# Rows of four transposes merged in pairs in a two-layer hybrid encoder kernel

## Chip, cores and metric

The kernel runs on one core of a Trainium2 chip. The metric is the device time of one execution in microseconds (us). Before the change the median of three runs is 1239.62 us (1239.03 to 1239.73).

## What is computed

Two layers of a macaron encoder on 256 tokens of width 1024, all in float32. Cut to what matters here:

```
for l in range(2):
    x = x + 0.5 * swiglu(rms_norm(x, g1), w1, w3, w2)
    h = rms_norm(x, gm);  z = h @ w_in
    y_na, y_gla, y_mla = three token mixers on slices of z
    mixed = sum_i sigmoid(gate_i) * (y_i @ w_br_i)
    x = x + mixed @ w_out
    x = x + 0.5 * swiglu(rms_norm(x, g2), w1, w3, w2)
```

Every product needs its left side with the contracted dimension on the partitions, so activations that were computed with tokens on the partitions are transposed in 128x128 blocks: x before each norm's product, the compressed inputs and the queries and keys inside the mixers, and `mixed` before `w_out`.

## The kernel before

**Split operands.** A float32 value is kept as a pair: a high part rounded to fp32r (made on ScalarE, ACT) and a low part, the rest (made on VectorE, DVE). A product is three passes of TensorE (PE): high x high, high x low, low x high. Weights arrive by DMA in units of 128x2048 and are split in halves of 128x1024: `emit_hi` (L143, ACT) and `emit_lo` (L149, DVE). The activations' pairs lie in `xT` (token block t, high or low, eight 128-wide blocks k).

**Tokens** come in two blocks, t = 0 and 1; a row of x is handled in halves of 512 columns, h = 0 and 1.

**Order.** No scheduler moves anything: every engine runs its instructions in the order in which the Python code emits them. `tick()` is called after each block of matmuls (most often 12 of 512 columns). It calls `fill()`, which emits pending weight splits, and then advances each live task (a Python generator) by one step; `spawn(gen, wait)` sets after how many ticks the task's first step comes, `yield n` sets the next. `finish(task)` emits what is left of it at once. With `tick(True)` the tasks come ahead of `fill()`. So a row of transposes that a task emits falls between two blocks of matmuls on PE, and its evictions fall behind the weight splits that ACT and DVE were given before.

**Transposes.** A row of four 128x128 transposes fills one PSUM bank (`tr_t`, tag `ta`, four banks shared with other uses). The rows that the change touches:

- `norm_task` (L257 to L277): one task for each half row of x. Four transposes (L264), four scaled copies into the high part (L267, ACT), four subtractions for the low part (L271, DVE), the sum of squares (L274). It stands at the end of each feed-forward block's last product (`wide_out`, x is updated at L554) and of the mixer's last product (x updated at L1229). Five norms run this way.
- `c_task` (L607 to L620): the transposes of the compressed inputs, one row for j = 0, one for j = 1, with a yield between them (L616).
- `na_tr` (L705 to L717): neighbourhood queries and keys, two rows each (L699).
- `mix_task` (L1206 to L1214): in `branch`, the third branch's product of block (h, t) is multiplied by its gate and added to `mixed` (L1200 and L1202, both on DVE for this branch); `mix_task` then transposes the block (L1211) and splits it into `xT` by `split_bank`: L247 on ACT, then L248 on DVE. The product with `w_out` (`wide_out`, `wide_burst`) follows at once. Its first 12 matmuls read block t = 0 of half h = 0: four with the high part, then two with the low part, and so on.

All products go through one helper, `mm` (L370), so the trace shows them under that line.

Of the kernel before, what the change touches and what calls it, by code (L numbers as in the profile page):

```python
# [6 lines left out]
F32 = mybir.dt.float32  # L7
# [3 lines left out]
AF = mybir.ActivationFunctionType  # L11
ALU = mybir.AluOpType
# [34 lines left out]
def body(tc, T):  # L47
# [3 lines left out]
    with ctx:  # L51
# [7 lines left out]
        PE, ACT, DVE, POOL = nc.tensor, nc.scalar, nc.vector, nc.gpsimd  # L59

        def s2(shape=(128, 512), dt=F32):
            return sp.tile(list(shape), dt, name="s2", tag="s2", bufs=S2_BUFS)

        def small(n, dt=F32, tag="sm", bufs=24):
            return sm.tile([128, n], dt, name=tag, tag=tag, bufs=bufs)

        def bank(tag, bufs):
            return pp.tile([128, 512], F32, name=tag, tag=tag, bufs=bufs)

        acc_t = lambda: bank("acc", 4)  # L70
        tr_t = lambda: bank("ta", 4)
# [90 lines left out]
        def unit():  # L162
            i = st["next"]
            st["next"] += 1
            split_to(2 * i + 3)
            return hls[i]
# [19 lines left out]
        def tick(fill_last=False):  # L186
            if not fill_last:
                fill()
            for tk in list(tasks):
                if tk.done:  # L190
                    continue
                tk.wait -= 1
                if tk.wait <= 0:
                    step(tk)
            if fill_last:
                fill()

        def spawn(gen, wait=1):
            tk = Task(gen, wait)
            tasks.append(tk)  # L200
            return tk

        def finish(tk):
            while not tk.done:
                step(tk)
# [7 lines left out]
        x = cst.tile([128, 2, D], F32, name="x")  # L213
        idt = cst.tile([128, 128], F32, name="idt")
        xT = cst.tile([128, 2, 2, 8, 128], F32R, name="xT")
# [27 lines left out]
        def junk(n):  # L243
            return sp.tile([128, 512], BF, name="junk", tag="junk", bufs=1)[:, :n]

        def split_bank(ps, hi, lo, n=512):
            ACT.activation(out=hi, in_=ps, func=AF.Copy)  # L247
            DVE.tensor_tensor(out=lo, in0=ps, in1=hi.bitcast(F32), op=ALU.subtract)  # L248
# [3 lines left out]
        rs_sq, rs_b, ss_x = {}, {}, {}  # L252

        def xdst(t, h):
            return [xT[:, t, w, 4 * h:4 * h + 4, :].rearrange("p k n -> p (k n)") for w in range(2)]

        def norm_task(t, h, G):  # L257
            sl = slice(h * 512, h * 512 + 512)
            if h == 0:
                ss_x[t] = small(2)  # L260
            yield 1
            ps = tr_t()
            for k in range(4):
                PE.transpose(ps[:, k * 128:(k + 1) * 128], x[:, t, h * 512 + k * 128:h * 512 + k * 128 + 128], idt)  # L264
            for k in range(4):
                kk = 4 * h + k
                ACT.activation(out=xT[:, t, 0, kk, :], in_=ps[:, k * 128:(k + 1) * 128], func=AF.Copy,  # L267
                               scale=G[:, kk:kk + 1])
            for k in range(4):
                kk = 4 * h + k  # L270
                DVE.scalar_tensor_tensor(out=xT[:, t, 1, kk, :], in0=ps[:, k * 128:(k + 1) * 128],  # L271
                                         scalar=G[:, kk:kk + 1], in1=xT[:, t, 0, kk, :].bitcast(F32),
                                         op0=ALU.mult, op1=ALU.subtract)
            ACT.activation(out=junk(512), in_=x[:, t, sl], func=AF.Square, accum_out=ss_x[t][:, h:h + 1])  # L274
            if h == 1:
                rs_tk[t] = spawn(rs_task(t))

        rs_tk = {}

        def rs_task(t):  # L280
            ss = ss_x[t]
            DVE.tensor_tensor(out=ss[:, 0:1], in0=ss[:, 0:1], in1=ss[:, 1:2], op=ALU.add)
            r = rs_x[t] = small(1)
            DVE.tensor_scalar(ss[:, 1:2], ss[:, 0:1], 1.0 / D, EPS, op0=ALU.mult, op1=ALU.add)  # L284
            POOL.tensor_tensor(out=r, in0=ss[:, 1:2], in1=mhalf[:, 0:1], op=ALU.pow)  # L285
            yield 1
            for count in (64, 256):
                q = rs_sq[t, count] = small(1)
                DVE.tensor_scalar(q, r, r, 1.0 / count, op0=ALU.mult, op1=ALU.mult)
# [274 lines left out]
        def mixer(l, norms, after, prefetch):  # L564
# [5 lines left out]
                                     op0=ALU.mult, op1=ALU.mult)  # L570
# [37 lines left out]
            def c_task(deps):  # L608
                for d in deps:
                    finish(d)  # L610
                yield 1
                for j in range(2):
                    ps = tr_t().rearrange("p (k t n) -> p k t n", k=2, t=2)
                    for t in range(2):
                        for k in range(2):
                            PE.transpose(ps[:, k, t, :], cn[t][:, j * 256 + k * 128:j * 256 + k * 128 + 128], idt)  # L616
                    hi, lo = s2(dt=F32R), s2(dt=F32R)
                    split_bank(ps.rearrange("p k t n -> p (k t n)"), hi, lo)
                    cT[j] = (hi, lo)
                    yield 1  # L620

            def ev_r(t, acc):
                r = rl[t] = small(160, tag="rl", bufs=2)
# [70 lines left out]
            def four(src, base):  # L694
                ps = tr_t().rearrange("p (k t n) -> p k t n", k=2, t=2)
                for t in range(2):
                    for k in range(2):
                        a = base + k * 128
                        PE.transpose(ps[:, k, t, :], src[t][:, a:a + 128], idt)  # L699
                return ps.rearrange("p k t n -> p k (t n)")  # L700
# [4 lines left out]
            def na_tr(nm, deps):  # L705
                for d in deps:
                    finish(d)
                yield 1
                for j in range(2):
                    ps = four([nqk[nm, 0], nqk[nm, 1]], j * 256)  # L710
                    o = naT[nm, j] = s2((128, 2, 256))
                    if nm == "q":
                        ACT.activation(out=o.rearrange("p k (c r) -> p k r c", r=4),
                                       in_=ps.rearrange("p k (r c) -> p k r c", r=4), func=AF.Copy, scale=gqk_na)
                    else:
                        DVE.tensor_copy(o, ps)
                    yield 1  # L717

            def na_chain(deps):
                for d in deps:  # L720
# [461 lines left out]
            mixed, mt = {}, {}  # L1182

            def branch(i, key):
                lh = lambda hl, k, t: yT[key, k // 2][hl][:, (k % 2) * 256 + t * 128:(k % 2) * 256 + t * 128 + 128]
                for h in range(2):
                    hl = unit()
                    for t in range(2):
                        acc = acc_t()
                        burst(acc, lh, hl, range(4), t, 512, True, True)  # L1190
                        if i < 2:
                            g = gates[:, t, i * 1024 + h * 512:i * 1024 + h * 512 + 512]
                        else:
                            g = late.pop((h, t))
                        if i == 0:
                            m = mixed[h, t] = s2()
                            DVE.tensor_tensor(out=m, in0=acc, in1=g, op=ALU.mult)
                        else:
                            m = mixed[h, t]
                            DVE.tensor_tensor(out=g, in0=acc, in1=g, op=ALU.mult)  # L1200
                            e = DVE if i == 2 else POOL
                            e.tensor_tensor(out=m, in0=m, in1=g, op=ALU.add)  # L1202
                        if i == 2:
                            mt[h, t] = spawn(mix_task(h, t), 3)
                        tick()

            def mix_task(h, t):
                m = mixed.pop((h, t))
                ps = tr_t()
                for k in range(4):  # L1210
                    PE.transpose(ps[:, k * 128:k * 128 + 128], m[:, k * 128:k * 128 + 128], idt)  # L1211
                split_bank(ps, *xdst(t, h))
                return
                yield  # L1214

# [18 lines left out]
        def spawner(ap, into, params_of=None):  # L1234
            G = []

            def f(t, h):
                into[t, h] = spawn(norm_task(t, h, G[0]), 1)

            def prefetch():  # L1240
                G.append(load_gain(ap))
                if params_of is not None:
                    load_params(params_of)
            return f, prefetch
# [3 lines left out]
        for l in range(DEPTH):  # L1248
            W = T["layers"][l]
            nm, n2 = {}, {}  # L1250
# [132 lines left out]
```

## Time and profile before

| | |
|---|---|
| median of three runs | 1239.62 us |
| profiled execution, its own time | 1239.52 us |
| its span in the trace | 1237.7 us |
| PE busy | 1233.5 us (100%) |
| DVE busy | 892.4 us (72%) |
| ACT busy | 710.9 us (57%) |
| POOL busy | 217.6 us (18%) |

A time of a run holds some 2 us around the span. The ends of matmuls are modelled, so a PE that shows 100% busy may still wait: a wait shows as a longer distance between starts, and on the row of the weight loads (PEld).

### The profile page before, as it was taken

The page shows a single profiled execution, that of the slowest core. Times are in us where ns is not written, and L with a number is a line of the kernel's source. Part 1 is how long each engine was busy: PE and PEld are TensorE (multiplying, and loading weights), DVE is VectorE, ACT ScalarE, POOL GpSimd, SP SyncE. Part 2 cuts the span into 40 slices and gives each one's busy share as a digit, 9 for nine tenths or more (in the row PEclk, how much of TensorE's full clock was granted, in tenths as well). Part 3 has the DMA queues.
Part 4 walks back from the last instruction along what each step waited for, and adds up shares of the span by engine and source line. Part 5 has one row for each costly group of instructions (what it writes and reads, how often), then busy time and mean ns, then how long its engine had stood idle before and what let it go on. Part 6 is the DMA issues. An engine that isn't in the chain of part 4 may idle for free.

```text
span 1237.7 us, 18188 instructions
## 1 busy us (share of the span) xinstructions
PE 1233.5 (100%) x7048; PEld 1061.4 (86%) x7048; DVE 892.4 (72%) x1399; ACT 710.9 (57%) x1317; POOL 217.6 (18%) x165
## 2 busy tenths in 40 slices
PE   9999999999999999999999999999999999999999
PEld 8888888889988888888888888888899888888887
DVE  6888837689667778886478886476896677788862
ACT  7665536567755465655356565356686654656541
POOL 0222102132112012220012220021322030122200
PEclk9999999999999999999999999999999999999999
DMA  8655744662554455557355556346525445555560
GB/s 332 211 202 177 252 150 162 224 195 93 187 190 146 173 200 178 201 177 249 119 204 207 191 195 247 108 172 238 176 99 201 171 142 190 188 195 189 186 238 34
DMA packets 37910, 228.58 MB, mean 185 GB/s; under 512 B 5760, under 2 KB 7040, under 8 KB 13376
## 3 DMA queue, kind: packets, MB, share of 16 engines
q1 hardware_dynamic: 37680, 227.42, 52.0%
q8 instruction: 55, 0.90, 0.3%
q14 instruction: 31, 0.25, 0.1%
q10 hardware_dynamic: 144, 0.00, 0.0%
HBM read 224.26 MB, written 1.05 MB: 182 GB/s over the span
## 4 chain that ended last, share of the span: by engine, by line
PE 100%; DVE 0%; issue 0%
PE acc L370 81%; PE ta L370 16%; PE ta L699 1%; PE ta L264 1%; PE ta L308 0%; PE ta L1211 0%; PE ta L684 0%; PE ta L737 0%; PE ta L616 0%; PE ta L1026 0%; PE ta L299 0%; PE ta L477 0%; PE ta L956 0%; DVE x L554 0%; DVE junk L305 0%
## 5 line engine op out<-in xcount | busy, mean ns | idle before, releaser
L149 DVE TENSOR_TENSOR hl<-raw,hl 128x1024 fp32r<-128x1024 f32 (+1 forms) x418 | 561.2, 1383 | 83.6 <-ACT hl L143 73.2
L143 ACT ACTIVATE hl<-raw 128x1024 fp32r<-128x1024 f32 (+1 forms) x418 | 412.8, 1040 | 103.4 <-PE ta L370 81.3
L370 PE MATMUL acc<-xT,hl 128*128 128x256 f32 (+1 forms) x2720 | 464.7, 332 | 0.0
L370 PEld LDWEIGHTS acc<-xT,hl 128*128 128x128 f32 x2720 | 407.6, 188 | 54.7
L370 PE MATMUL acc<-hl,xT 128*128 128x512 f32 (+1 forms) x1584 | 362.1, 384 | 0.0
L370 PEld LDWEIGHTS acc<-hl,xT 128*128 128x128 f32 x1584 | 291.9, 188 | 47.7 <-issue 1.7
L370 PE MATMUL acc<-hl,s 128*128 128x512 f32 x816 | 193.6, 390 | 0.0
L370 PEld LDWEIGHTS acc<-hl,s 128*128 128x128 f32 x816 | 152.5, 188 | 31.7 <-issue 0.3
L491 POOL TENSOR_TENSOR s<-s,rsb 128x512 f32<-128x512 f32 x79 | 109.5, 1387 | 352.4 <-DVE s L490 352.4
L370 PE MATMUL ta<-hl,s 128*128 128x512 f32 (+2 forms) x648 | 148.3, 378 | 0.0
L370 PEld LDWEIGHTS ta<-hl,s 128*128 128x128 f32 x648 | 117.6, 188 | 21.7
L500 ACT ACTIVATE s<-s 128x256 fp32r<-128x256 f32 x82 | 34.0, 417 | 168.2 <-DVE s L498 168.2
L490 DVE TENSOR_TENSOR s<-acc,s 128x256 f32<-128x256 f32 x158 | 59.7, 420 | 58.4 <-ACT s L489 58.4
L577 POOL TENSOR_TENSOR sm<-sm,mhalf 128x4 f32<-128x4 f32 (+2 forms) x24 | 36.7, 1531 | 192.0 <-DVE sm L581 192.0
L285 POOL TENSOR_TENSOR sm<-sm,mhalf 128x1 f32<-128x1 f32 x12 | 14.1, 1176 | 294.3 <-DVE sm L284 294.3
L489 ACT ACTIVATE s<-acc 128x256 f32<-128x256 f32 x158 | 50.6, 372 | 0.0
L248 DVE TENSOR_TENSOR s<-ta,s 128x512 fp32r<-128x512 f32 (+1 forms) x46 | 26.6, 604 | 30.0 <-ACT s L247 29.9
L267 ACT ACTIVATE xT<-ta,gain 128x128 fp32r<-128x128 f32 x80 | 22.8, 368 | 36.3 <-PE ta L264 36.3
L247 ACT ACTIVATE s<-ta 128x512 fp32r<-128x512 f32 (+1 forms) x46 | 22.9, 532 | 31.4 <-PE ta L699 16.9
L496 ACT ACTIVATE s<-s 128x256 f32<-128x256 f32 x82 | 34.2, 419 | 11.3 <-POOL s L491 0.3
L370 PE MATMUL ta<-s,s 64*64 64x128 f32 (+4 forms) x720 | 35.8, 260 | 0.0
L370 PEld LDWEIGHTS ta<-s,s 64*64 64x64 f32 (+3 forms) x720 | 30.4, 145 | 5.9 <-issue 4.2
(164 smaller groups left out, 676.6 us busy)
## 6 DMA issues: line engine op xcount, KB each, us to landing
raw<-in_l_f_w SPq DMA_DIRECT2D x123, 1024.0 KB, 4.8
raw<-in_l_in_g SPq DMA_DIRECT2D x16, 816.0 KB, 4.4
raw<-in_l_in_late SPq DMA_DIRECT2D x8, 1024.0 KB, 4.8
raw<-in_l_out SPq DMA_DIRECT2D x8, 1024.0 KB, 4.7
raw<-in_l_f_up SPq DMA_DIRECT2D x6, 1024.0 KB, 4.8
raw<-in_l_in_m SPq DMA_DIRECT2D x4, 1024.0 KB, 4.8
raw<-in_l_in_gr SPq DMA_DIRECT2D x4, 1024.0 KB, 4.8
raw<-in_l_in_r SPq DMA_DIRECT2D x4, 1024.0 KB, 4.8
```

The source lines that it names most:

```text
L143: ACT.activation(out=hls[j][:, 0, sl], in_=raws[j][:, sl], func=AF.Copy)
L149: DVE.tensor_tensor(out=hl[:, 1, sl], in0=r[:, sl], in1=hl[:, 0, sl].bitcast(F32), op=ALU.subtract)
L247: ACT.activation(out=hi, in_=ps, func=AF.Copy)
L248: DVE.tensor_tensor(out=lo, in0=ps, in1=hi.bitcast(F32), op=ALU.subtract)
L267: ACT.activation(out=xT[:, t, 0, kk, :], in_=ps[:, k * 128:(k + 1) * 128], func=AF.Copy, scale=G[:, kk:kk + 1])
L370: PE.matmul(out=out, lhsT=lhsT, rhs=rhs, start=start, stop=stop, skip_group_check=True)
L489: ACT.activation(out=g[:, j, :], in_=a[j][:, 256:], func=AF.Copy)
L490: DVE.tensor_tensor(out=g[:, j, :], in0=a[j][:, :256], in1=g[:, j, :], op=ALU.add)
L491: POOL.tensor_tensor(out=g, in0=g, in1=rb[:, None, :].to_broadcast([128, 2, 256]), op=ALU.mult)
L496: ACT.activation(out=g[:, 0, :], in_=g[:, 0, :], func=AF.Silu)
L500: ACT.activation(out=o[:, 0, :], in_=g[:, 0, :], func=AF.Copy)
L577: POOL.tensor_tensor(out=r[:, :n], in0=ss[:, :n], in1=mhalf[:, :n], op=ALU.pow)
```

## The change

Eighteen pairs of rows become rows of eight. In `norm_task` one task does both halves of a token block: eight transposes, then the evictions of both banks, then both sums of squares (five norms, two token blocks: ten pairs). In `c_task` the yield between the two rows goes (one pair a layer), in `na_tr` that of the queries (one pair a layer). In `mix_task` one task does both token blocks of a half h; it is spawned when t = 1 is done (two pairs a layer). No instruction is added or removed; the order on the engines changes.

```diff
-        def norm_task(t, h, G):
+        def norm_task(t, G):
...
-            ps = tr_t()
-            for k in range(4):
-                PE.transpose(ps[:, k * 128:(k + 1) * 128], x[:, t, h * 512 + k * 128:h * 512 + k * 128 + 128], idt)
...
+            pss = [tr_t() for _ in range(2)]
+            for h in range(2):
+                for k in range(4):
+                    PE.transpose(pss[h][:, k * 128:(k + 1) * 128],
+                                 x[:, t, h * 512 + k * 128:h * 512 + k * 128 + 128], idt)
+            for h, ps in enumerate(pss):
...
@@ c_task
                     cT[j] = (hi, lo)
-                    yield 1
+                yield 1
@@ na_tr
-                    yield 1
+                    if nm == "k" or j:
+                        yield 1
@@ branch
-                        if i == 2:
-                            mt[h, t] = spawn(mix_task(h, t), 3)
+                        if i == 2 and t:
+                            mt[h, 0] = mt[h, 1] = spawn(mix_task(h), 3)
@@ mix_task
-            def mix_task(h, t):
-                m = mixed.pop((h, t))
-                ps = tr_t()
-                for k in range(4):
-                    PE.transpose(ps[:, k * 128:k * 128 + 128], m[:, k * 128:k * 128 + 128], idt)
-                split_bank(ps, *xdst(t, h))
+            def mix_task(h):
+                pss = [tr_t() for _ in range(2)]
+                for t in range(2):
+                    m = mixed.pop((h, t))
+                    for k in range(4):
+                        PE.transpose(pss[t][:, k * 128:k * 128 + 128], m[:, k * 128:k * 128 + 128], idt)
+                for t in range(2):
+                    split_bank(pss[t], *xdst(t, h))
@@ spawner
             def f(t, h):
-                into[t, h] = spawn(norm_task(t, h, G[0]), 1)
+                if h:
+                    into[t, 0] = into[t, 1] = spawn(norm_task(t, G[0]), 1)
```

The changed file's lines are shifted: L370 becomes L372, L1200 and L1202 become L1203 and L1205, L1211 becomes L1215, L264 becomes L263.

PE around `mix_task`, before, from the last six matmuls of the third branch's block (h = 1, t = 0). The rows `acc<-hl,s` are the branch's product, the rows `acc<-hl,xT` the product with `w_out`, and `s_3748`, `s_3820`, `s_3839`, `s_3865` are the blocks of `mixed` for (h, t) = (0, 0), (0, 1), (1, 0), (1, 1).

```order
993 L370 MATMUL acc<-hl,s_3903 128x512 x2
994 L370 MATMUL acc<-hl,s_3904 128x512
995 L1211 MATMUL ta<-idt,s_3748 128x128 x4
996 L370 MATMUL acc<-hl,s_3894 128x512 x2
...
1003 L370 MATMUL acc<-hl,s_3904 128x512
1004 L1211 MATMUL ta<-idt,s_3820 128x128 x4
1005 L370 MATMUL acc<-hl,xT 128x512 x12
1006 L1211 MATMUL ta<-idt,s_3839 128x128 x4
1007 L370 MATMUL acc<-hl,xT 128x512 x12
1008 L1211 MATMUL ta<-idt,s_3865 128x128 x4
1009 L370 MATMUL acc<-hl,xT 128x512 x48
```

The same place now:

```order
998 L372 MATMUL acc<-hl,s_3904 128x512
999 L1215 MATMUL ta<-idt,s_3748 128x128 x4
1000 L1215 MATMUL ta<-idt,s_3820 128x128 x4
1001 L372 MATMUL acc<-hl,xT 128x512 x24
1002 L1215 MATMUL ta<-idt,s_3839 128x128 x4
1003 L1215 MATMUL ta<-idt,s_3865 128x128 x4
1004 L372 MATMUL acc<-hl,xT 128x512 x60
```

The transposes of block (0, 0) stood 12 matmuls ahead of the first product that reads them; now only the four of block (0, 1) stand between.

DVE at the same place, before. L1200 and L1202 are the gate's product and the sum of `mixed`, L149 the weight splits, L248 the low parts of the transposed blocks.

```order
364 L1200 TENSOR_TENSOR s_3666<-acc,s_3666 128x512
365 L1202 TENSOR_TENSOR s_3839<-s_3839,s_3666 128x512
366 L248 TENSOR_TENSOR xT<-ta,xT 128x512
367 L1200 TENSOR_TENSOR s_3728<-acc,s_3728 128x512
368 L1202 TENSOR_TENSOR s_3865<-s_3865,s_3728 128x512
369 L149 TENSOR_TENSOR hl<-raw,hl 128x1024 x2
370 L248 TENSOR_TENSOR xT<-ta,xT 128x512 x2
371 L149 TENSOR_TENSOR hl<-raw,hl 128x1024 x2
372 L248 TENSOR_TENSOR xT<-ta,xT 128x512
```

And now:

```order
362 L1203 TENSOR_TENSOR s_3666<-acc,s_3666 128x512
363 L1205 TENSOR_TENSOR s_3839<-s_3839,s_3666 128x512
364 L1203 TENSOR_TENSOR s_3728<-acc,s_3728 128x512
365 L1205 TENSOR_TENSOR s_3865<-s_3865,s_3728 128x512
366 L149 TENSOR_TENSOR hl<-raw,hl 128x1024 x2
367 L248 TENSOR_TENSOR xT<-ta,xT 128x512 x2
368 L149 TENSOR_TENSOR hl<-raw,hl 128x1024 x2
369 L248 TENSOR_TENSOR xT<-ta,xT 128x512 x2
```

The low part of block (0, 0) moved from ahead of the last L1200 to behind it, its L1202 and two weight splits.

DVE at a norm (the first layer's mixer norm), now. L556 is the update of x (L554 before), L272 the low parts (L271 before), L284 and L286 the start of the inverse root mean square.

```order
116 L556 SCALAR_TENSOR_TENSOR x<-acc,x 128x512 x2
117 L149 TENSOR_TENSOR hl<-raw,hl 128x1024 x2
118 L556 SCALAR_TENSOR_TENSOR x<-ta,x 128x512
119 L272 SCALAR_TENSOR_TENSOR xT<-ta,gain,xT 128x128 x8
120 L149 TENSOR_TENSOR hl<-raw,hl 128x1024
121 L556 SCALAR_TENSOR_TENSOR x<-ta,x 128x512
122 L284 TENSOR_TENSOR sm<-sm 128x1
...
127 L272 SCALAR_TENSOR_TENSOR xT<-ta,gain,xT 128x128 x8
```

Before, the low parts came four at a time, the first four right behind the first L554 pair; now the eight of a token block stand together, those of t = 0 ahead of the last update of x.

## Rows read from the trace of the kernel before

**Rows 1.** The page: busy time, granted clock in slices, chain by engine.

```profile
PE 1233.5 (100%) x7048; PEld 1061.4 (86%) x7048; DVE 892.4 (72%) x1399; ACT 710.9 (57%) x1317; POOL 217.6 (18%) x165
PEclk9999999999999999999999999999999999999999
PE 100%; DVE 0%; issue 0%
```

**Rows 2.** Timeline, PE, first mixer norm: start, length, engine, line, shapes, count.

```profile
183.64 0.60 PE L264 MATMUL ta<-idt,x 128*128 128x128 f32 x4
184.00 3.02 PE L370 MATMUL ta<-hl,s 128*128 128x512 f32 x12
186.85 0.60 PE L264 MATMUL ta<-idt,x 128*128 128x128 f32 x4
...
190.05 0.60 PE L264 MATMUL ta<-idt,x 128*128 128x128 f32 x4
...
193.26 0.60 PE L264 MATMUL ta<-idt,x 128*128 128x128 f32 x4
```

**Rows 3.** Timeline, PE, blocks of matmuls with no transposes between them.

```profile
256.36 2.88 PE L370 MATMUL ta<-hl,s 128*128 128x512 f32 x12
259.08 5.61 PE L370 MATMUL acc<-hl,xT 128*128 128x512 f32 x24
```

**Rows 4.** Timeline, PE, a row of eight, and the next row of four.

```profile
391.30 1.03 PE L699 MATMUL ta<-idt,s 128*128 128x128 f32 x8
392.09 16.59 PE L370 MATMUL acc<-hl,s 128*128 128x512 f32 x72
408.51 0.60 PE L1211 MATMUL ta<-idt,s 128*128 128x128 f32 x4
```

**Rows 5.** Timeline, all engines, first layer's mix; in brackets idle time and releaser.

```profile
411.71 0.60 PE L1211 MATMUL ta<-idt,s 128*128 128x128 f32 x4
411.91 0.69 DVE L1200 TENSOR_TENSOR s<-acc,s 128x512 f32<-128x512 f32 x1 [0.17 <-PE acc L370]
...
412.35 0.60 ACT L247 ACTIVATE xT<-ta 128x512 fp32r<-128x512 f32 x1 [2.60 <-PE ta L1211]
412.71 0.69 DVE L1202 TENSOR_TENSOR s<-s,s 128x512 f32<-128x512 f32 x1
...
413.32 2.35 DVE L149 TENSOR_TENSOR hl<-raw,hl 128x1024 fp32r<-128x1024 f32 x2
...
415.28 3.18 PE L370 MATMUL acc<-hl,xT 128*128 128x512 f32 x12
...
415.59 1.30 DVE L248 TENSOR_TENSOR xT<-ta,xT 128x512 fp32r<-128x512 f32 x2
...
416.33 1.70 PEld L370 LDWEIGHTS acc<-hl,xT 128*128 128x128 f32 x8 [0.31 <-DVE xT L248]
...
418.30 0.60 PE L1211 MATMUL ta<-idt,s 128*128 128x128 f32 x4
...
429.67 0.60 PE L264 MATMUL ta<-idt,x 128*128 128x128 f32 x4
```

**Rows 6.** The same view, second layer's mix.

```profile
1026.67 0.69 DVE L1200 TENSOR_TENSOR s<-acc,s 128x512 f32<-128x512 f32 x1 [0.17 <-PE acc L370]
...
1031.08 1.68 PEld L370 LDWEIGHTS acc<-hl,xT 128*128 128x128 f32 x8 [0.31 <-DVE xT L248]
```

**Rows 7.** Timeline, ACT and DVE, first mixer norm.

```profile
184.28 1.14 ACT L267 ACTIVATE xT<-ta,gain 128x128 fp32r<-128x128 f32 x4 [4.82 <-PE ta L264]
...
185.45 1.13 DVE L271 SCALAR_TENSOR_TENSOR xT<-ta,gain,xT 128x128 fp32r<-128x128 f32 x4 [0.92 <-ACT xT L267]
...
190.40 1.21 DVE L149 TENSOR_TENSOR hl<-raw,hl 128x1024 fp32r<-128x1024 f32 x1
191.53 0.68 DVE L554 SCALAR_TENSOR_TENSOR x<-ta,x 128x512 f32<-128x512 f32 x1
```

**Rows 8.** Timeline, PE, the first matmuls of the program.

```profile
1.17 3.60 PE L308 MATMUL ta<-junk 128*128 128x512 bf16 x8 [1.17 <-DVE junk L305]
```

More of the change, by code (lines that the diff above doesn't have):

```diff
@@ L255, in xdst @@
             return [xT[:, t, w, 4 * h:4 * h + 4, :].rearrange("p k n -> p (k n)") for w in range(2)]
-        def norm_task(t, h, G):
-            sl = slice(h * 512, h * 512 + 512)
-            if h == 0:
-                ss_x[t] = small(2)
+        def norm_task(t, G):
+            ss_x[t] = small(2)
             yield 1
-            ps = tr_t()
-            for k in range(4):
-                PE.transpose(ps[:, k * 128:(k + 1) * 128], x[:, t, h * 512 + k * 128:h * 512 + k * 128 + 128], idt)
-            for k in range(4):
[L266 to L276, printed above, removed]
@@ new lines, in norm_task @@
+            pss = [tr_t() for _ in range(2)]
[5 more added lines that the diff above has]
+                for k in range(4):
+                    kk = 4 * h + k
+                    ACT.activation(out=xT[:, t, 0, kk, :], in_=ps[:, k * 128:(k + 1) * 128], func=AF.Copy,
+                                   scale=G[:, kk:kk + 1])
+                for k in range(4):
+                    kk = 4 * h + k
+                    DVE.scalar_tensor_tensor(out=xT[:, t, 1, kk, :], in0=ps[:, k * 128:(k + 1) * 128],
+                                             scalar=G[:, kk:kk + 1], in1=xT[:, t, 0, kk, :].bitcast(F32),
+                                             op0=ALU.mult, op1=ALU.subtract)
@@ L278, in body @@
+            for h in range(2):
+                ACT.activation(out=junk(512), in_=x[:, t, h * 512:h * 512 + 512], func=AF.Square,
+                               accum_out=ss_x[t][:, h:h + 1])
+            rs_tk[t] = spawn(rs_task(t))
         rs_tk = {}
@@ L1202, in branch @@
                             e.tensor_tensor(out=m, in0=m, in1=g, op=ALU.add)
-                        if i == 2:
-                            mt[h, t] = spawn(mix_task(h, t), 3)
+                        if i == 2 and t:
+                            mt[h, 0] = mt[h, 1] = spawn(mix_task(h), 3)
                         tick()
-            def mix_task(h, t):
-                m = mixed.pop((h, t))
-                ps = tr_t()
-                for k in range(4):
-                    PE.transpose(ps[:, k * 128:k * 128 + 128], m[:, k * 128:k * 128 + 128], idt)
-                split_bank(ps, *xdst(t, h))
+            def mix_task(h):
+                pss = [tr_t() for _ in range(2)]
+                for t in range(2):
+                    m = mixed.pop((h, t))
+                    for k in range(4):
+                        PE.transpose(pss[t][:, k * 128:k * 128 + 128], m[:, k * 128:k * 128 + 128], idt)
+                for t in range(2):
+                    split_bank(pss[t], *xdst(t, h))
                 return
```

## The prediction

> **What bounds the kernel now.** I read the page first: PE is busy for 1233.5 us of a span of 1237.7 us, the chain of waits is PE for 100%, and the granted clock stands at full in all 40 slices [rows 1]. DVE (72%) and ACT (57%) have room on average. So the time is the length of PE's instruction stream, and the change can act in two ways only: it makes that stream shorter, or it makes PE wait. Neither shows in busy time, because ends of matmuls are modelled. I therefore took the timeline of PE and measured from start to start, then the timeline of all engines where PE reads what was just transposed.
>
> The ordinary pitch: 12 matmuls of 512 columns from 256.36 to 259.08 take 2.72 us, 0.2267 us each [rows 3]. At the first mixer norm three periods of four transposes and 12 matmuls last from 183.64 to 193.26, 9.62 us [rows 2]; 36 matmuls are 8.16 us, so **a row of four costs (9.62 - 8.16) / 3 = 0.49 us**. A row of eight exists too: from its start to that of the next row, with 72 matmuls between them, 408.51 - 391.30 = 17.21 us pass [rows 4], less 16.32 us: **a row of eight costs 0.89 us**. Two rows of four are 0.97 us, so each merged pair shortens PE's stream by 0.08 us. The reason that the rows suggest is a fixed price for changing over to transposes and back.
>
> **The change part by part.** *Pairs.* There are 18: ten in the five norms, two for the compressed inputs, two for the neighbourhood queries, four in the mix. 18 x 0.08 = 1.4 us less. The bounds: a lower price for the second row follows from the distance from a row's start to the next matmul, 0.36 us for four [rows 2] and 0.79 us for eight [rows 4], so four transposes alone are 0.43 us and what a pair can save by this is 0.49 - 0.43 = 0.06 us, 1.1 us in all; and 0 if the price of the changeover is not saved. I take 0.08, because it is measured over whole periods.
>
> The Trainium skill (TensorE: Matmul & The Clock Gate, Part 4) puts a 128x128 bf16 transpose at about 390 ns alone and 275 ns inside a kernel. If the head of each row cost that difference, 18 rows fewer would give an estimated 2.1 us in place of 1.4, and the total below would be 0.7 us lower; the rows here are float32 in a stream, and I keep the measured figure.
>
> *Norms.* In the new order one block of 12 matmuls, not two, lies between the transposes of t = 0 and the mixer's first product. Worked out from the first mixer norm: the row at 183.64 [rows 2] is gone, so the next block ends at 183.64 + 2.72 = 186.36 and eight transposes follow, to 187.25; the last block of the product runs to 189.97, the mixer's first block to 192.69, and there the eight of t = 1 are due. ACT begins 0.64 us after a row's start and needs 1.14 us for four (184.28 against 183.64 [rows 2, 7]), so its eight run from 187.00 to 189.28. DVE takes four in 1.13 us, behind ACT's four as at 185.45 [rows 7]: 188.14 to 189.27 and 189.28 to 190.41. PE reads the first high part at 189.97 and the first low part two matmuls later, at 190.42; the blocks of h = 0 are there 1.1 us or more ahead. Then DVE has a split of 1.21 us and the update of x of 0.68 us [rows 7], to 192.3; the eight of t = 1 need that x at 192.69. **0.4 us of room**, the thinnest cover of the change. For t = 1 a block of 12 matmuls lies between again, and the same sum leaves its low parts ahead of their reader. I cost the norms at no wait; if that cover were gone, the price is in the rivals. The sums of squares come later behind eight copies, but their reader, the inverse root, is needed only after 24 more matmuls.
>
> *Compressed inputs and queries.* Each second row is moved ahead by 12 matmuls (2.7 us). Its reader is an up-projection or the attention stage, 48 or more matmuls later (11 us), against 0.6 us of ACT and 0.7 us of DVE for a bank (the lengths in rows 5). No wait. Nothing is added to a DMA queue or to POOL, and no DMA is moved.
>
> *Mix, half h = 0.* This is the place that decides. Before, the transposes of block (0, 0) stood 12 matmuls ahead of the product with w_out; now they stand right in front of it. The product's first four matmuls want the high part, from the fifth on the low part. The low part is an L248 on DVE, and in the new order it stands behind the last L1200, its L1202 and two weight splits. The old trace times exactly this chain, for block (1, 0)'s neighbour: L1200 starts at 411.91, L1202 at 412.71, the splits at 413.32, L248 at 415.59, and PE's weight load that waited for it goes at 416.33 [rows 5]: **4.42 us** from L1200 to PE; in the second layer 1031.08 - 1026.67 = 4.41 us [rows 6]. There PE paid little, as 12 matmuls and a row lay before the reading block.
>
> In the new order the row at 408.51 [rows 4] is gone, so the branch's last block ends at 408.51 + 2.72 = 411.23 and the eight transposes start. L1200 starts 0.20 us after that point (411.91 against 411.71 [rows 5]), at 411.43, and PE's fifth load goes at 411.43 + 4.42 = 415.85. From such a load to the end of its block the old trace needs 418.30 - 416.33 = 1.97 us [rows 5], so the block ends at 417.82. Without a wait it would end at 411.23 + 0.89 + 2.72 = 414.84. **The wait is 2.98 us in each layer.** The high part comes from ACT, which has nothing else then: 0.64 + 0.60 us after the row's start, 412.47, some 0.4 us late for the first matmul, but those four matmuls end long before 415.85, so this lies inside the wait. From above: if PE waited for both L248, 1.30 us and not one, it would be some 0.6 us more. From below: without the two splits in front (2.27 us from 413.32 to 415.59) 0.71 us would stay; but DVE runs in the order shown, so I take 2.98.
>
> What goes: before, the four rows and 84 matmuls from 408.51 to 429.67 took 21.16 us [rows 4, 5]; less 19.04 for the matmuls and 4 x 0.49 for the rows, the old wait for L248 cost 0.17 us. So the mix adds 2.98 - 0.17 = 2.81 us a layer, 5.6 us. Half h = 1 has 24 matmuls (5.4 us) between its eight transposes and its reader, and DVE has only two splits (2.35 us) and two L248 (1.30 us) ahead: no wait. Afterwards PE has nothing to regain, since it shows no wait of this size that could shrink.
>
> **Sum:** -1.4 + 5.6 = +4.2 us on the profiled execution's 1239.52 us: **1243.7 us**, 0.34% slower. That execution lies 0.1 us under the median of the three runs, so the same number stands for the median.
>
> **The rivals.**
> *The clock falls in the wait* (chance 0.12). Transposes, four matmuls and 2.5 us of nothing could bring the granted clock to its lower level. The trace shows no such wait after its start and full clock everywhere, so it speaks neither way. The program's first eight matmuls stretch over 3.6 us, 0.45 us each, 0.22 us over the pitch [rows 8, 3]: if eight matmuls a layer ran so, 2 x 8 x 0.22 = 3.5 us more, 1247.2 us. The Trainium skill (same page, "Why this matters for your kernels", and Part 4) says that idle gaps between bursts bring the clock back down and that transposes do not count as matmul activity; no wait in this trace tests it.
> *The second row of eight in a norm waits for x* (0.07). It decides where DVE is over 0.4 us later than worked out, for example because its splits start later. A shortfall as large as the margin, 0.4 us at five norms, gives 2 us more: 1245.7 us.
> *The pairs save nothing* (0.08). For: the row of eight was measured at one place. Then 1239.52 + 5.6 = 1245.1 us.
> *Not slower: the low part is not behind the splits in time* (0.06). If DVE were through its two splits by the time L1202 ends, 0.71 us would stay of the wait: 2 x (0.71 - 0.17) - 1.4 = -0.3 us, 1239.2 us. It decides from 2.3 us of slack on DVE between the branch's block and its end. Against: DVE's idle time there is 0.17 us [rows 5], and the order puts the splits first.
>
> **How the numbers follow.** The forecast as such has 0.67, and its own range is 1243.1 to 1245.1 us (pairs from 1.1 to 1.5 us, the wait from 2.7 to 3.5 us). With the cases of pairs that save nothing and of the norms the range 1242.4 to 1246.4 us holds 8 in 10; the clock and the other side stay out. A measurement of this kernel tells about 0.2% (2.5 us) from no change. Slower by more than that: all cases but the last, less a little for a wait half as long, 0.91; within 0.2%: 0.07; faster: 0.02, for pairs that save several times what I measured with a wait that never comes.
>
> **What would show it.** In the changed trace PE's weight loads wait for L248's DVE row some 2.5 us in each layer, at the fifth matmul of the product with w_out, with the two splits right ahead of it on DVE; the old 0.31 us waits are gone. Rows of eight cost about 0.89 us, and the stretches from norm to mix are shorter by 0.08 us a pair. The granted clock stays full. It would be wrong if L248 ran ahead of the splits, if PE waited at the second eight of a norm, or if the rows of eight cost twice a row of four.

## The result and the profile after

The changed kernel took 1248.94 us (median of four executions, 1247.87 to 1249.24) against 1239.32 us for the kernel before on the same chips: ratio 1.0077, 95% interval 1.0064 to 1.0090. It is slower by 9.6 us, more than twice the forecast 4.2 us, and outside the range. One execution further down, a fourth of the version with transposes in the wait, took 1356.98 us at a mean granted clock of 0.851; it left no trace and stays out of every comparison.

The page of the profiled execution (1249.24 us, span 1247.5 us), the lines that answer to [rows 1]:

```profile
PE 1238.3 (99%) x7048; PEld 1065.2 (85%) x7048; DVE 892.7 (72%) x1399; ACT 711.3 (57%) x1317; POOL 217.5 (17%) x165
PEclk9999999999999999999999999999999999999999
PE 99%; DVE 0%; issue 0%; DMA 0%; ACT 0%; DVEq 0%
```

Every engine has as many instructions as before. The span grew by 9.8 us and PE's busy time by 4.8 us: PE waits more, and it also takes longer for the same matmuls. The slices of 31 us in the page's row of the clock hide this.

**The wait in the mix** is where it was forecast. The timeline of all engines at the first layer's mix of the changed kernel, the place of [rows 5]:

```profile
411.07 1.04 PE L1215 MATMUL ta<-idt,s 128*128 128x128 f32 x8
411.27 0.69 DVE L1203 TENSOR_TENSOR s<-acc,s 128x512 f32<-128x512 f32 x1 [0.29 <-PE acc L372]
411.71 1.09 ACT L247 ACTIVATE xT<-ta 128x512 fp32r<-128x512 f32 x2 [6.76 <-PE ta L1215]
412.07 0.69 DVE L1205 TENSOR_TENSOR s<-s,s 128x512 f32<-128x512 f32 x1
412.36 0.76 PEld L372 LDWEIGHTS acc<-hl,xT 128*128 128x128 f32 x4 [0.49 <-ACT xT L247]
...
412.68 2.35 DVE L149 TENSOR_TENSOR hl<-raw,hl 128x1024 fp32r<-128x1024 f32 x2
...
414.95 1.28 DVE L248 TENSOR_TENSOR xT<-ta,xT 128x512 fp32r<-128x512 f32 x2
...
415.68 6.03 PEld L372 LDWEIGHTS acc<-hl,xT 128*128 128x128 f32 x20 [2.57 <-DVE xT L248]
415.69 6.46 PE L372 MATMUL acc<-hl,xT 128*128 128x512 f32 x20 [2.13 <-DVE xT L248]
...
421.98 1.04 PE L1215 MATMUL ta<-idt,s 128*128 128x128 f32 x8
```

Read down the DVE rows: L1203, L1205, the two splits, L248, and only then PE's fifth weight load. From L1203's start to that load 415.68 - 411.27 = 4.41 us pass, against 4.42 and 4.41 in the old trace [rows 5, 6].

**The clock.** The 20 matmuls behind the wait last 6.46 us, where 20 at the ordinary pitch take 4.5 us. The same trace in stretches; the columns are busy time and count for PE, PEld, DVE, ACT and POOL, then the granted clock, the DMA share and GB/s:

```profile
410.00:415.00 5.00, 3.30 (x18) 2.29 (x16) 4.50 (x7) 2.97 (x4) 0.00 (x0) 1.00 0.64 211
415.00:420.00 5.00, 4.31 (x12) 3.42 (x13) 3.50 (x5) 0.00 (x0) 0.00 (x0) 0.66 0.70 231
420.00:425.00 5.00, 5.00 (x28) 4.16 (x27) 1.60 (x3) 2.38 (x4) 0.00 (x0) 1.00 0.48 192
...
1035.00:1040.00 5.00, 3.80 (x12) 3.00 (x13) 4.02 (x5) 0.20 (x1) 0.00 (x0) 0.76 0.59 210
1040.00:1045.00 5.00, 5.00 (x26) 4.18 (x25) 1.25 (x2) 1.88 (x3) 0.00 (x0) 0.90 0.58 210
```

The mean of 0.66 is a mixture of the full level (2.4 GHz) and the half (1.2 GHz): shortly after PE resumed, the granted clock stood at half and then rose again, in both layers. Read start by start, seven of the 20 matmuls lie 426 or 427 ns apart, where the ordinary distance is 227.

**A slower feed-forward block.** The chain of waits in the second layer's first feed-forward block, before and after (start, length, engine, line, count). The piece holds the 608 matmuls of the block's first products that stand behind a row of six transposes, and the first 12 of the next product:

```profile
638.75 108.14 PE acc L370 x620
```

```profile
642.60 110.16 PE acc L372 x620
```

The same 620 matmuls take 2.02 us longer at full clock and without a wait. In the three other feed-forward blocks the mean distance between starts is the same in the two kernels.

**The norms** held. The timeline at the first mixer norm of the changed kernel, the place of [rows 2, 7]:

```profile
186.48 1.03 PE L263 MATMUL ta<-idt,x 128*128 128x128 f32 x8
...
187.12 2.18 ACT L268 ACTIVATE xT<-ta,gain 128x128 fp32r<-128x128 f32 x8 [6.59 <-PE ta L263]
...
188.30 2.16 DVE L272 SCALAR_TENSOR_TENSOR xT<-ta,gain,xT 128x128 fp32r<-128x128 f32 x8 [0.78 <-ACT xT L268]
...
191.50 0.68 DVE L556 SCALAR_TENSOR_TENSOR x<-ta,x 128x512 f32<-128x512 f32 x1
...
192.82 1.04 PE L263 MATMUL ta<-idt,x 128*128 128x128 f32 x8
```

The x of t = 1 is ready at 192.18, 0.6 us ahead of the second eight. Between the two rows lie 24 matmuls (5.44 us) of 6.34 us: a row of eight costs 0.90 us here, as forecast. In the old trace the same stretch, two rows of four and 24 matmuls, took 190.05 - 183.64 = 6.41 us [rows 2], 0.07 us more.

### The profile page after: what moved, and what is told of

It reads as the page before. It is cut to its first block, busy times and chain, and to the rows that moved or that the text cites. A ratio compares the mean times of both kernels' runs of the same rounds, so it can differ in the third digit from the quotient of the medians.

```text
span 1247.5 us, 18199 instructions
## 1 busy us (share of the span) xinstructions
PE 1238.3 (99%) x7048; PEld 1065.2 (85%) x7048; DVE 892.7 (72%) x1399; ACT 711.3 (57%) x1317; POOL 217.5 (17%) x165
## 4 chain that ended last, share of the span: by engine, by line
PE 99%; DVE 0%; issue 0%; DMA 0%; ACT 0%; DVEq 0%
PE acc L372 80%; PE ta L372 16%; PE ta L701 1%; PE ta L263 1%; PE ta L740 0%; PE ta L686 0%; DMA gcol<-in_gcol 0%; DVE hl L149 0%; PE ta L1215 0%; PE ta L301 0%; PE ta L1029 0%; PE ta L618 0%; DVE s L1203 0%; PE ta L479 0%; DVE xT L248 0%
## 5 line engine op out<-in xcount | busy, mean ns | idle before, releaser
L149 DVE TENSOR_TENSOR hl<-raw,hl 128x1024 fp32r<-128x1024 f32 (+1 forms) x418 | 561.2, 1382 | 93.3 <-ACT hl L143 83.5
L372 PE MATMUL acc<-xT,hl 128*128 128x256 f32 (+1 forms) x2720 | 466.8, 333 | 0.0
L372 PEld LDWEIGHTS acc<-xT,hl 128*128 128x128 f32 x2720 | 408.6, 188 | 55.8
L372 PE MATMUL acc<-hl,xT 128*128 128x512 f32 (+1 forms) x1584 | 362.1, 385 | 4.8 <-DVE xT L248 4.3
L372 PEld LDWEIGHTS acc<-hl,xT 128*128 128x128 f32 x1584 | 295.1, 189 | 54.3 <-DVE xT L248 5.1
L372 PE MATMUL acc<-hl,s 128*128 128x512 f32 x816 | 193.0, 390 | 0.0
L372 PEld LDWEIGHTS acc<-hl,s 128*128 128x128 f32 x816 | 152.6, 188 | 31.9 <-issue 0.3
L372 PE MATMUL ta<-hl,s 128*128 128x512 f32 (+2 forms) x648 | 147.9, 378 | 0.0
L372 PEld LDWEIGHTS ta<-hl,s 128*128 128x128 f32 x648 | 117.8, 188 | 21.7
L248 DVE TENSOR_TENSOR s<-ta,s 128x512 fp32r<-128x512 f32 (+1 forms) x46 | 26.5, 604 | 16.4 <-ACT s L247 16.3
L372 PE MATMUL ta<-s,s 64*64 64x128 f32 (+4 forms) x720 | 35.8, 260 | 0.0
L372 PEld LDWEIGHTS ta<-s,s 64*64 64x64 f32 (+3 forms) x720 | 30.4, 145 | 5.9 <-issue 4.2
```

The lines of the kernel that those rows point to most:

```text
L149: DVE.tensor_tensor(out=hl[:, 1, sl], in0=r[:, sl], in1=hl[:, 0, sl].bitcast(F32), op=ALU.subtract)
L372: PE.matmul(out=out, lhsT=lhsT, rhs=rhs, start=start, stop=stop, skip_group_check=True)
```

## The experiments

All times are device time; the kernel before, run beside them, had medians of 1239.10 to 1239.41 us.

### The changed kernel again

No edit.

> The changed kernel, a second time. Theory: its 9.6 us over the kernel before are 5.6 us of waiting in the two mixes, 3.2 us because the granted clock stands at half for some matmuls after each wait, 2.0 us because the second layer's first feed-forward block runs at 176.7 ns a matmul instead of 173.4, less 1.3 us for the merged pairs. If the slower pitch belongs to this program it is there again and the time is 1247.5 to 1249.5. Rival: the pitch differs from execution to execution; then a look without it gives about 1247.

Measured 1245.38 us. The wait is there, the clock did not fall, and the slow block is there. Its 20 matmuls behind the wait, the same stretch, and its slow block in the chain:

```profile
415.04 4.83 PE L372 MATMUL acc<-hl,xT 128*128 128x512 f32 x20 [2.13 <-DVE xT L248]
```

```profile
415.00:420.00 5.00, 4.96 (x23) 4.10 (x24) 2.85 (x3) 0.00 (x0) 0.00 (x0) 1.00 0.83 259
```

```profile
640.33 110.16 PE acc L372 x620
```

So the clock's part varies from execution to execution, and the slow block is in both traces. The expectation was right on the block and took the falls for granted, so it missed the time. 6.46 - 4.83 = 1.6 us is what one fall costs. The mean granted clock counts the falls where no trace was kept: 0.997 in the three executions of 1248.74 to 1249.24 us, one of which is the trace above with two falls; 0.999 in that of 1247.87 us, which makes one fall; 1.0 here.

### The mix alone

```diff
-                            mt[h, t] = spawn(mix_task(h, t), 3)
+                        if i == 2 and t:
+                            mt[h, 0] = mt[h, 1] = spawn(mix_task(h), 3)
...
```

in the kernel before, with the changed `mix_task`.

> The kernel before, with the mix's rows alone merged. Theory: both waits and both falls of the clock are here, 2 x (2.8 + 1.6) us, less 4 pairs of 0.07: about 1239.3 + 8.5 = 1247.8; the granted clock falls after each mix. Rival, that the norms' merging causes the fall or the slow pitch: then full clock and 1239.3 + 5.3 = 1244.6, with feed-forward blocks at the ordinary pitch.

Measured 1247.67 us (1245.54 to 1247.87), ratio 1.0064 (1.0051 to 1.0078). The granted clock is 0.67 between 415 and 420 us of the profiled execution, mean 0.997 in three executions and 0.999 in the one of 1245.54 us. The 620 matmuls take 108.14 us:

```profile
415.00:420.00 5.00, 4.05 (x11) 3.20 (x12) 3.76 (x5) 0.00 (x0) 0.00 (x0) 0.67 0.75 229
...
643.10 108.14 PE acc L370 x620
```

So the mix carries wait and clock, and it does not carry the slow block.

### Everything but the mix

The changed kernel with `branch` and `mix_task` of the kernel before.

> The changed kernel with the mix's rows as before: 14 pairs merged. Theory: no new wait, full clock, 14 x 0.07 = 1.0 us less than before: 1238.3; 1240.3 if the slow pitch of the second layer's first feed-forward block comes from the merged norms. Rival, that merged norms cost by themselves: 1241 or more with waits at the second row of eight of a norm.

Measured 1240.18 us (1239.84 to 1240.66), ratio 1.0008 (0.9999 to 1.0017), clock 1.0 in all eleven executions. The slow block is there:

```profile
637.80 110.16 PE acc L372 x620
```

The merges outside the mix thus bring in the 2.0 us.

### Ten matmuls in the wait

```diff
-        def wide_burst(acc, lhs, u, hl, t, start, stop):
+        def wide_burst(acc, lhs, u, hl, t, start, stop, cover=False):
...
+                if cover and kk == 0:
+                    ps = tr_t()
+                    for _ in range(10):
+                        mm(ps, hl[:, 0, :128], hl[:, 0, :512], True, True)
```

on for u = 0, t = 0 of the product with w_out; the ten results are read by nobody.

> The changed kernel with ten matmuls that nobody reads put where PE waits for the low part (behind the fourth matmul of the product with w_out, each layer). The wait stays, but PE is not idle in it. Theory: the fall of the clock comes from the idle stretch, so the clock stays full and the time is 3.2 us less than the changed kernel's: 1245.7. Rival, that the clock falls for another reason (the transposes, the load of the program): it falls again and the time stays at about 1249.

Measured 1245.64 us (1245.33 to 1245.92), clock 1.0 in all four executions. The timeline shows PE at work until L248 is done, and the 20 matmuls at the ordinary pitch:

```profile
412.99 2.43 PE L372 MATMUL ta<-hl 128*128 128x512 f32 x10
...
415.28 4.87 PE L372 MATMUL acc<-hl,xT 128*128 128x512 f32 x20
```

```profile
415.00:420.00 5.00, 5.00 (x23) 3.82 (x22) 3.09 (x4) 0.00 (x0) 0.00 (x0) 1.00 0.81 246
```

The stretch in which PE did nothing is what brought the clock down. By the mean clock of each execution, it fell in 7 of the 10 waits of the changed kernel, the second execution included, in 7 of 8 with the mix alone, and in none of 8 here.

### Transposes in the wait

As above with `for _ in range(21): PE.transpose(ps[:, :128], idt, idt)`.

> As the kernel with ten filling matmuls, but with 21 transposes of the identity in their place, which take PE as long. Theory, that what matters is whether PE runs at all: full clock, 1245.6. Rival, that transposes do not count as activity for the clock: it falls in some of the executions as without filling, 1247 to 1249.

Measured 1245.72 us, the median of three executions (1245.45 to 1246.27), each at a mean granted clock of 1.0. The first layer's wait in the profiled one, and the clock behind it:

```profile
413.61 2.46 PE L462 MATMUL ta<-idt 128*128 128x128 f32 x21
...
415.00:420.00 5.00, 5.00 (x28) 4.21 (x27) 3.72 (x5) 0.00 (x0) 0.00 (x0) 1.00 0.74 231
```

In the three none of six waits was followed by a fall. Here a row of float32 transposes kept the clock up as matmuls did.

### Low parts ahead of the splits

```diff
-                        tick()
+                        tick(i == 2 and h == 1 and t == 1)
```

in `branch` of the changed kernel: the last tick does its tasks before the weight splits.

> The changed kernel with the evictions of the mix's first eight transposes ahead of the two weight splits on ACT and DVE (the last tick of the third branch does its tasks before the splits). Theory: of the wait of 2.98 us some 0.7 stays, and the clock stays full as PE is idle for under a microsecond: 1239.2 + 2 x (0.7 - 0.17) - 1.3 + 2.0 for the slow pitch = 1241.0. Rival, that the wait comes from elsewhere (the high part, a bank, the weights): it stays at 1245 to 1249.

Measured 1240.89 us (1240.63 to 1241.11), ratio 1.0015 (1.0005 to 1.0024), clock 1.0. The first layer's mix:

```profile
410.39 1.04 PE L1215 MATMUL ta<-idt,s 128*128 128x128 f32 x8
...
411.99 1.28 DVE L248 TENSOR_TENSOR xT<-ta,xT 128x512 fp32r<-128x512 f32 x2
...
412.73 4.42 PEld L372 LDWEIGHTS acc<-hl,xT 128*128 128x128 f32 x20 [0.29 <-DVE xT L248]
```

PE's load follows L248 at once, 2.34 us (412.73 - 410.39) behind the start of the row of eight; in the changed kernel it is 4.61 us (415.68 - 411.07) behind it. The difference, 2.27 us, is as long as the two splits. The place of the two splits in DVE's order is the cause of most of the wait; what is left, with the slow block still in, makes the 1.6 us over the kernel before.

### One norm back in halves

The kernel without the mix's merges, with the norm of the second layer's first feed-forward block as before (`norm_task` in halves for that one caller).

> All merges but the mix's and those of one norm, that of the second layer's first feed-forward block. Theory: the slow pitch of that block (176.7 ns a matmul against 173.4, 2.0 us) hangs on what stands on PE ahead of its long run of matmuls, so with that norm in rows of four again the pitch is 173.4 and the time 1239.2 - 12 x 0.07 = 1238.4. Rival, that the slow pitch comes from a merge farther up (compressed inputs, queries, other norms): it stays, 1240.3.

Measured 1238.16 us (1237.82 to 1238.70), ratio 0.9992 (0.9983 to 1.0002), and the block is at the ordinary pitch:

```profile
637.77 108.14 PE acc L393 x620
```

### Two more transposes ahead of the block

```diff
-                    rs_bcast(1 if first is None else 3)
+                    rs_bcast(2 if first is None else 3)
```

in the kernel without the mix's merges.

> All merges but the mix's, and two more transposes (the same ones a second time) in the row that stands in each later feed-forward block right ahead of the long run of matmuls. Theory, that the slow pitch is locked in by how PE comes out of that row: the row's new length changes it; 173.4 ns and 1240.2 - 2.0 + 3 x 0.22 = 1238.9 if it falls the other way. Rival, that the pitch is set by the load on ACT, DVE or the weights in that block: it stays at 176.7, 1240.8.

Measured 1238.94 us (1238.38 to 1239.28), against 1240.18 without the edit, although three blocks have two transposes more:

```profile
638.41 108.14 PE acc L372 x620
```

### That norm alone

The kernel before with only the norm of the second layer's first feed-forward block merged.

> The kernel before with one norm merged, that of the second layer's first feed-forward block (two pairs of eighteen). Theory: that merge alone puts the block on the pitch of 176.7 ns: 1239.3 - 2 x 0.07 + 2.0 = 1241.2. Rival, that the slow pitch needs the other merges too (where PE stands after all of them): 173.4 ns and 1239.2.

Measured 1239.23 us (1238.64 to 1239.44), and 620 matmuls in 108.14 us. The theory fell here: that merge is needed for the slow block in this program, but it does not bring it about by itself.

### A shift at the program's start

`WARM = 9` for 8 in the kernel without the mix's merges.

> All merges but the mix's, with nine instead of eight warm-up matmuls at the program's start (0.4 us). It asks what keeps the second layer's first feed-forward block on the slow pitch. Theory, that the local exit from the row of transposes right ahead of the block decides, by some nanoseconds: a shift far ahead changes nothing, 176.7 ns and about 1240.6. Rival, that the place of PE's instructions in the whole stream decides: one pair more moves it and the pitch can be 173.4, about 1238.6.

Measured 1240.79 us, one execution; the block stays slow:

```profile
638.39 110.16 PE acc L372 x620
```

A shift of everything by one matmul from the program's start does not switch the block. The three versions of the changed kernel that were edited in the mix (ten matmuls, transposes, low parts first) kept it too.

### The mix's second half merged

`mix_task` for h = 0 in two rows of four as before, for h = 1 merged, with that norm in halves.

> The merges that cost nothing together: four norms, compressed inputs, queries, and of the mix the second half h = 1 alone, which has 24 matmuls between its transposes and its reader; 14 pairs. Theory: no wait, full clock, ordinary pitch in all feed-forward blocks, 1239.3 - 14 x 0.07 = 1238.3, under both kernels. Rival, that the merged half of the mix makes PE wait too: 1240 or more.

Measured 1239.27 us (1238.93 to 1239.62), ratio 1.0002 (0.9993 to 1.0011): 1.1 us more than with no merge in the mix, of which the two mixes make 0.8 us between the two traces. The rival was right. The row of (1, 0), now gone from between the first two blocks of the product with w_out, had been cover for the low part of block (0, 1):

```profile
415.72 2.11 PE L393 MATMUL acc<-hl,xT 128*128 128x512 f32 x8 [0.33 <-DVE xT L248]
```

Waits of PEld for this L248 sum to 1.5 us in the two layers; in the kernel before they were 0.31 us each [rows 5, 6]. In the changed kernel this cost does not show: PE resumes only when the first half's L248 is done, and the second is over before it is read.

### Both together

The kernel above, with the last tick's tasks ahead of the splits.

> The kernel of 14 cheap merges with the mix's second half merged, and now the last low part of half h = 0 ahead of the weight splits (the third branch's last tick does its tasks first). Theory: the wait of 0.66 us a layer that this half's merge had left goes, with the 0.17 us of the kernel before: 1239.2 - 14 x 0.07 - 2 x 0.17 = 1237.9 at the ordinary pitch. Rival, that the delayed weight splits are late for the product with w_out: 1239 or more with PE waiting for L149.

Measured 1238.00 us (1237.51 to 1238.55), ratio 0.9989 (0.9980 to 0.9998). It is the only version whose interval lies under the kernel before, by a tenth of a percent or 1.4 us. No load waits for an L248 of `xT` any more; the first 24 matmuls of the product run through:

```profile
411.43 5.74 PE L393 MATMUL acc<-hl,xT 128*128 128x512 f32 x24
417.01 1.03 PE L1238 MATMUL ta<-idt,s 128*128 128x128 f32 x8
```

## Why the prediction was right on the wait and wrong on the time

- *Pairs, 18 x 0.08 = 1.4 us less:* right in kind, a little too much. Between the traces of the kernel before and of the one without the mix's merges, equal matmuls move together by 0.92 us over the 14 pairs outside the mix, 0.066 us each, between the prediction's 0.06 and 0.08. The four pairs in the mix cannot be read apart from the wait; at the same price 18 make 1.2 us.
- *Norms, compressed inputs and queries at no wait:* right; 0.6 us of room where 0.4 had been worked out.
- *The wait in the mix, 2.98 us a layer:* right. Without the clock's fall, in the second execution, the first layer's two rows of eight start at 410.42 and 419.71; 9.29 us less 24 matmuls (5.44) and a row (0.89) is 2.96 us. The low-parts-first version confirms the mechanism.

```profile
410.42 1.04 PE L1215 MATMUL ta<-idt,s 128*128 128x128 f32 x8
...
419.71 1.03 PE L1215 MATMUL ta<-idt,s 128*128 128x128 f32 x8
```

- *The clock:* the rival happened. Its price, 3.5 us for two falls, is close to the 3.2 us measured, in part by luck: the count of eight slow matmuls came from the program's start, and nothing in the old trace tied it to a wait. Its chance of 0.12 was the mistake, since in the changed kernel and with the mix alone such a wait ended in a fall 14 times of 18. That the trace "speaks neither way" was true and no reason for a small chance. The Trainium skill (TensorE: Matmul & The Clock Gate, "Why this matters for your kernels") warns of idle gaps between bursts of matmuls; the traces agree that a gap brings the clock down, with 0.66 granted in the stretch behind one of 2.1 us on PE, which is shorter than the gaps that the page warns of.
- *"The change can act in two ways only: it makes that stream shorter, or it makes PE wait":* this is the step that failed. The same matmuls took longer, twice over: at half clock (3.2 us), and in one feed-forward block at full clock (2.0 us). The first stood outside the sum, as a rival with a small chance; the second had no term and no rival.

Together: -1.2 + 2 x (2.96 - 0.17) + 3.2 + 2.0 = 9.6 us, against 9.6 us measured. The runs show the parts one by one: without the falls 1245.38 us, without the mix 1240.18 us, without the mix and with one norm in halves 1238.16 us.

**What stays open.** In the slow block the distances between starts repeat over six matmuls (113, 232, 118, 241, 120, 236 ns; a mean of 176.7), in the ordinary one over four (113, 232, 118 and 230 or 231 ns; a mean of 173.4). All feed-forward blocks of all kernels begin in the pattern of six, and the row of six transposes that follows normally ends it: the first layer's first block goes on in a pattern of two (117, 230 ns) with the same mean, the others in that of four. In the changed program one block stays in the pattern of six. The first two matmuls behind the row lie 316 ns apart there, and 313 or 314 in its other blocks; over all traces it is 315 to 317 ns in slow blocks and 312 to 315 in the others, so this distance alone does not tell them apart. The edit of the row itself switched the block back, a shift at the program's start did not, and the one merged norm is needed in this program but not enough. What decides it, in the state of PE or elsewhere, was not found.

## What to carry to other kernels

Transposes that sit between blocks of matmuls are also cover for the evictions of those before them: count, for each row that moves, how many matmuls are left until its first reader, and which older instructions stand ahead of its eviction on DVE. A wait like this one, 2.1 us of nothing on PE in a kernel that is bound by TensorE, should be priced with the clock's fall behind it, 1.6 us here, as the likely case; filling it with idle matmuls kept the clock but left the wait. Where a change of a tenth of a percent is at stake, compare the distances between equal matmuls block by block, since the pitch itself can move.

## What was not expected of the hardware

- A mixed stream of matmuls of 512 and 256 columns ran at either of two steady pitches, 173.4 and 176.7 ns, the same in both traces of one program, and a row of transposes can switch between them.
- The Trainium skill (TensorE: Matmul & The Clock Gate, Part 4) says that transposes do not count as PE-busy in the same way, and that the full clock does not engage for them. With 21 float32 transposes in the wait a clock that stood at full stayed there in three executions, six waits; the measurement decides for this case, and no run here shows whether transposes can bring the clock up.
- The fall of the clock behind the same wait is not certain: two, one or none in an execution of the same program, so that its times spread from 1245.38 to 1249.24 us.
